# A list scheduler's cost model: landing times that grow with a transfer's size, and time between dependent instructions of one engine

## The chip, the cores and the metric

One core of one Trainium2 chip runs the whole program in one launch. The metric is the device time of that launch in microseconds (us), the median over runs. Engines: PE is TensorE (matmuls), DVE is VectorE, ACT is ScalarE, POOL is GpSimd, and SP is the engine whose queue issues every DMA of this kernel.

## The reference

One layer of a hybrid backbone on 128 context and 1024 latent tokens (1152 rows, NT), model width 1024:

```
mod = silu(c) @ w_mod + b_mod              # 6 x 1024 values: shift, scale, gate of both halves; for c and c_ctx
h   = rmsnorm(x) * (1 + scale_a) + shift_a
z   = h @ w_in                              # 3456 columns: r k v, decay/a/gate LoRA (1920), and 3 x 512 for the convolution
y   = forward and backward RWKV-7 scan (8 heads x 64), group norm, bonus, gate g
oc  = rmsnorm(gate_b * conv3(gate_c * hc))
x1  = x + gate_a * (concat(y, oc) @ w_out)
h2  = rmsnorm(x1) * (1 + scale_f) + shift_f
x2  = x1 + gate_f * (relu(h2 @ w_ff1)**2 @ w_ff2)     # width 4096
out = rmsnorm(x2) * final_g, and the context's final scan states
```

## The kernel before, in words

All the kernel's instructions are emitted through the class `Order`, which is a list scheduler that runs while the program is built. Each piece of work is a generator (a task); an operation that it emits carries the engines it may run on, a modelled duration for each, and the tiles it reads and writes. `start` (L83 to L93) works out the earliest start of an operation from the log of earlier accesses to the same boxes of tiles, adding a latency `HOP` for every pair of different engines; `issue` (L189 on) books it and logs its end plus a `tail`. The scheduler then always takes the operation that can start first, priorities deciding between near-equals. What comes out is one fixed instruction order for each engine, and for a few copies and scalings (`cp`, `mul`, `lin`) also the engine. On the chip each engine runs its order strictly in sequence, with real waits. A model that is wrong therefore costs time as an order in which an instruction stands too early (the engine stands still at it, with everything behind it) or too late.

Of the model, three places matter here: `start`, where an earlier access by the same engine costs nothing; `act` (L335 to L340), an activation's duration from its size; and `dma` (L449 to L451), which books 1.5 us of the queue for 512 KB and a tail of 1900 ns whatever the size.

The program's stages, with the times of the profiled execution:

- A, 0 to 66 us: modulation for the first norm (`mod_in_task`), norm and transposition of x into `hT` (`h_task`).
- B, 66 to 519 us: the input projection. `proj_task` walks over 27 blocks of 128 columns and three groups of 384 rows, 24 matmuls `bank<-hT,w` each. Beside it `front_task`, `value_task`, `kk_task` and `gate_task` turn the results, mostly on DVE and ACT, into scan operands that SP stores to DRAM (`qr_d`, `kb_d`, `kt_d`, `v_d`, `fin_d`). `mod_task` computes the other 32 blocks of the modulation: for each, a load of 512 KB into the only tile `wm`, 16 recorded matmuls `bank<-wm,sc` (eight in the code, in two passes each), a copy to `R`, a small matmul `bank<-sel,R` and an addition; after the last, two copies to `gc`, a transposition, a copy, and the store `gate_d`. The next load of `wm` cannot start before the matmuls on the last one are through.
- C, 519 to 935 us: the scan. `load_task` loads slots (`bk`, `qr`, `V`, `bkT`) of scan operands, `prep_worker` and `chain_task` run short matmuls on 64 x 64 blocks with DVE and ACT between them, `finish_task` normalises (loading `fg` and `f1` from `fin_d`). Its tiles take the place of those of B.
- D, 935 to 1056 us: the output projection (`oproj_task`), and `x1_task`: gate, residual, norm, and eight transpositions `bank<-ident,mx` per tile of 128 rows, each four followed by four `lin` (L400) to `h` on ACT.
- E, 1056 to 1800 us: both matmuls of the MLP.
- Tail, 1800 to 1865 us: the last accumulation of the MLP, and `y_task` per tile of 128 rows: two evacuations `facc<-bank,facc`, times `late` (the gate), plus `late` (x1), a square with accumulation on ACT, `Ln`, `Exp`, and the final scaling (`stt`, L377) with a store.

Of the kernel before, what the change touches and what calls it, by code (L numbers as in the profile page):

```python
# [27 lines left out]
class Order:  # L28
# [9 lines left out]
    HOP = {("pe", "dve"): 205.0, ("pe", "act"): 205.0, ("dve", "pe"): 145.0, ("act", "pe"): 175.0,  # L38
           ("act", "dve"): 150.0, ("dve", "act"): 130.0, ("act", "pool"): 170.0, ("pool", "dve"): 80.0,
           ("dve", "pool"): 150.0, ("pool", "act"): 110.0, ("pool", "pe"): 150.0}  # L40
    SLACK = 20.0
    GLUE = -1.0
    LOAD = 1290.0
# [38 lines left out]
    def start(self, eng, bi, bo, pe=None):  # L82
        t = 0.0  # L83
        if pe:

            t = self.sub + pe[1] * (1 if self.warm(self.sub) else 2)
            t = max([t] + [self.tiles[x] for x in pe[4]])
        for wr, bs in ((False, bi), (True, bo)):
            for nm, p0, p1, f0, f1 in bs:
                for q0, q1, g0, g1, te_, en, w in self.log.get(nm, ()):  # L90
                    if (wr or w or nm in self.banks) and p0 < q1 and q0 < p1 and f0 < g1 and g0 < f1 and en != eng:
                        t = max(t, te_ + self.HOP.get((en, eng), 70.0))
        return t  # L93

    def emit(self, opts, outs, ins, fn, tail=0.0, pe=None, table=None):
# [154 lines left out]
    def run(self, tasks):  # L250
# [3 lines left out]
        while self.tasks:  # L254
# [24 lines left out]
            if not cand:  # L279
# [3 lines left out]
            s0, eng = f.ready[0], f.ready[1]  # L283
            t = min((t for t in cand if t.ready[1] == eng and t.ready[0] <= s0 + self.SLACK),
                    key=lambda t: (t.prio, t.ready[0], t.n))
# [8 lines left out]
            if r != t.ready or n != t.next:  # L294
                t.ready, t.next = r, n
                if r[1] != eng or r[0] > s0 + self.SLACK:
                    continue
# [12 lines left out]
def kernel(  # L310
# [8 lines left out]
    te, ve, se, ge, sy = nc.tensor, nc.vector, nc.scalar, nc.gpsimd, nc.sync  # L319

    od = Order()

    def size(ap):
        n = 1
        for _, c in ap.ap[1:]:
            n *= c
        return n

    def in_psum(ap):
        return ap.space == PSUM  # L330

    def aps(*xs):
        return [x for x in xs if isinstance(x, bass.AP)]

    def act(out, in_, func=AF.Copy, **kw):  # L335
        x = aps(kw.get("scale"), kw.get("bias"))
        d = (52 if in_psum(in_) else 94) + 47 * len(x) + size(in_) / 1.2
        od.emit([("act", d)], [out] + aps(kw.get("accum_out")), [in_] + x,
                lambda e: se.activation(out=out, in_=in_, func=func, **kw),  # L339
                table=TABLES.get(func))  # L340
# [98 lines left out]
    def mm(out, lhsT, rhs, start=True, stop=True, **kw):  # L439
        pe_op(out, lhsT, rhs, lambda e: te.matmul(out, lhsT=lhsT, rhs=rhs, start=start, stop=stop, **kw))  # L440
# [7 lines left out]

    def dma(out, in_):  # L449
        n = size(out) * 4 * out.ap[0][1]  # L450
        od.emit([("dma", max(480.0, n / 350.0))], [out], [in_], lambda e: sy.dma_start(out=out, in_=in_), 1900.0)  # L451

    def split(src, hi, lo, eng="dve"):

# [8 lines left out]
    p1 = ctx.enter_context(tc.tile_pool(name="p1", bufs=1))  # L463
# [30 lines left out]
    for b in bank_t:  # L494
        nm = od.box(b)[0]
# [170 lines left out]
    def split_task():  # L666
        for i in range(2):
            dma(raws[i], w_in[0, :, blocks[i] * 128:(blocks[i] + 1) * 128].rearrange("(k p) c -> p k c", p=128))
        for i, cb in enumerate(blocks):
            if i >= 2:  # L670
                yield lambda: nproj[0] >= i - 1
            w2, raw = w2s[i % 2], raws[i % 2]
            for q in range(4):
                sl = slice(2 * q, 2 * q + 2)
                act(w2[:, 0, sl], raw[:, sl])
                tt(w2[:, 1, sl], raw[:, sl], w2[:, 0, sl].bitcast(F32), ALU.subtract)
            count(nsplit)
            yield
            if i + 2 < len(blocks):
                c2 = blocks[i + 2]  # L680
                dma(raw, w_in[0, :, c2 * 128:(c2 + 1) * 128].rearrange("(k p) c -> p k c", p=128))
# [17 lines left out]
    with tc.tile_pool(name="p0w", bufs=1) as pw, tc.tile_pool(name="p0", bufs=1) as p0:  # L699
# [9 lines left out]
        def par_task(g):  # L709
            r = 0  # L710
            for nm, ap, n in groups[g]:
                src = {"rk": "o (n h) q -> (o n) (h q)", "cw": "o t (n q) -> (o t n) q"}.get(nm, "o (n q) -> (o n) q")
                src = ap.rearrange(src, h=2) if nm == "rk" else ap.rearrange(src, q=128)
                dma(prs[g][r:r + n, :], src)
                r += n
# [5 lines left out]
            if g == 0:  # L721

                for w, nm in ((0, "c"), (1, "cctx")):
                    cv = prm[:, rows[nm]:rows[nm] + 8]
                    t = der[:, 50:58] if w == 0 else der[:, 42:50]
                    act(t, cv, AF.Tanh, scale=0.5)
                    tsc(t, t, 0.5, ALU.mult, 0.5, ALU.add)
                    tt(sc[:, :, w], t, cv, ALU.mult)
                mark(ready, "sc")
            else:  # L730
                yield lambda: "sc" in ready

                r0 = rows["mu"]
                tsc(der[:, 0:15], prm[:, r0:r0 + 15], -1.0, ALU.mult, 1.0, ALU.add)
                tsc(der[:, 15:30], prm[:, r0:r0 + 15], 0.5, ALU.mult)
                r0 = rows["w0_f"]
                tsc(der[:, 30:46], prm[:, r0:r0 + 16], 0.5, ALU.mult)
                r0 = rows["ka"]
                tsc(der[:, 58:62], prm[:, r0:r0 + 4], 0.5, ALU.mult)
                tsc(der[:, 62:66], prm[:, r0:r0 + 4], -0.5, ALU.mult, 1.0, ALU.add)  # L740
                for t, f, b in ((lw_w, w_w2_f, w_w2_b), (lw_a, w_a2_f, w_a2_b)):
                    dma(t[0:64], f[0])
                    dma(t[64:128], b[0])
                dma(lw_g, w_g2[0])
# [13 lines left out]
        def x_task():  # L758
            for i in range(TT):
                dma(xs_t[i], x_rows(i))  # L760
            for a, b in ((0, 5), (5, 9)):
                for i in range(a, b):
                    act(junk, xs_t[i], AF.Square, accum_out=ss[:, 0, i:i + 1])
                act(ss[:, 1, a:b], ss[:, 0, a:b], AF.Ln, scale=1.0 / D, bias=eps[:, 2:3])
                act(ss[:, 1, a:b], ss[:, 1, a:b], AF.Exp, scale=-0.5)
                for i in range(a, b):
                    tsc(xs_t[i], xs_t[i], ss[:, 1, i:i + 1], ALU.mult, eng=("dve", "pool"))
                    mark(ready, ("x", i))
                yield
# [1028 lines left out]
```

## Time and profile before

| what | value |
|---|---|
| median of three runs | 1871.28 us (1868.84, 1871.28, 1874.59) |
| the profiled execution | 1867.13 us, of which the span of the trace is 1865.3 us |
| granted clock of TensorE, mean | 0.981 |
| busy PE / DVE / ACT / POOL | 1725.0 / 1170.3 / 572.9 / 36.0 us |
| share of the 16 DMA engines taken by the queue of SP | 34.5 % |

Busy times are of the span of 1865.3 us. The profiled execution was 4.15 us below the median, so sums that are made against the trace are carried to the median as differences. PE is at work for 92 % of the span, but that is an average over stages: in E it never stops, and in A, in C, at the seams between the stages and in the tail other things end last. Matmul records are modelled, and a few can be missing.

### The profile page before, as it was taken

Reading aid. Unit: us, or ns where it says so; the run is one execution under the profiler, and the core shown is the slowest. Engines: PE = TensorE matmul, PEld = TensorE weight load, DVE = VectorE, ACT = ScalarE, POOL = GpSimd, SP = SyncE. Lnnn points to the kernel's source line nnn. Section 1 sums busy time; section 2 is a strip of 40 time slices with the busy share of each in tenths; the row PEclk is TensorE's granted clock in tenths of the full one; section 3 lists DMA queues with packets and bytes.
Section 4 is the critical chain, followed back from the end, with each engine's and each line's share of the span. In section 5 each row is a group of like instructions: output and inputs, shape, how many; then the busy total and the mean of one; then the engine's idle time right before and its main releaser. Section 6 shows DMA issues by size and latency. Waiting matters only on the chain.

```text
span 1865.3 us, 47366 instructions
## 1 busy us (share of the span) xinstructions
PE 1725.0 (92%) x20250; PEld 1535.8 (82%) x20250; DVE 1170.3 (63%) x2481; ACT 572.9 (31%) x1384; POOL 36.0 (2%) x167
## 2 busy tenths in 40 slices
PE   5899999999877878888989999999999999999996
PEld 3788888988767777777767899999999999999995
DVE  3557676777668877777655534555555555555557
ACT  5444344544244444444334421111100010000112
POOL 6000000000000000000000000000000000000000
PEclk9999999999999999999999999999999999999998
DMA  8436666665544443334144311111111111101142
GB/s 297 112 103 161 167 168 162 157 181 137 135 139 134 143 115 101 101 108 126 58 146 131 102 57 46 46 46 46 46 46 46 45 35 46 38 24 42 46 151 97
DMA packets 291449, 190.35 MB, mean 102 GB/s; under 512 B 109171, under 2 KB 274214, under 8 KB 291238
## 3 DMA queue, kind: packets, MB, share of 16 engines
q1 hardware_dynamic: 291238, 187.32, 34.5%
q8 instruction: 159, 2.61, 0.6%
q14 instruction: 52, 0.43, 0.1%
HBM read 137.44 MB, written 49.82 MB: 100 GB/s over the span
## 4 chain that ended last, share of the span: by engine, by line
PE 72%; DVE 8%; DMA 7%; issue 4%; ACT 4%; SPq 3%; DVEq 0%; ACTq 0%; POOL 0%; POOLq 0%
PE bank L440 72%; SPq L451 3%; DMA wm<-in_w_mod_dram 3%; DVE facc L362 1%; PE bank L443 1%; DMA fg<-fin_d 1%; DVE facc L377 1%; DVE x L362 1%; DVE y L362 1%; ACT mx L339 0%; ACT late L339 0%; DMA raw<-o_d 0%; ACT h L400 0%; DVE mx L362 0%; DMA late<-x_d 0%
## 5 line engine op out<-in xcount | busy, mean ns | idle before, releaser
L440 PE MATMUL bank<-hT,w 128*128 128x384 f32 (+1 forms) x2232 | 448.6, 354 | 0.0
L440 PEld LDWEIGHTS bank<-hT,w 128*128 128x128 f32 x2232 | 395.7, 191 | 26.8 <-issue 10.3
L440 PE MATMUL bank<-h,w 128*128 128x384 f32 x2304 | 409.9, 339 | 0.0
L440 PEld LDWEIGHTS bank<-h,w 128*128 128x128 f32 x2304 | 407.3, 188 | 1.2
L440 PE MATMUL bank<-w2f,f1f 128*128 128x512 f32 x1674 | 385.2, 389 | 0.0
L440 PEld LDWEIGHTS bank<-w2f,f1f 128*128 128x128 f32 x1674 | 314.0, 188 | 64.7
L362 DVE TENSOR_TENSOR facc<-bank,facc 128x512 f32<-128x512 f32 x252 | 173.9, 690 | 134.3 <-PE bank L440 133.1
L339 ACT ACTIVATE rl<-bank 128x384 f32<-128x384 f32 x96 | 47.2, 492 | 340.4 <-PE bank L440 340.4
L362 DVE TENSOR_TENSOR rl<-rl 128x384 f32<-128x384 f32 x96 | 53.4, 557 | 154.9 <-ACT rl L339 154.8
L440 PE MATMUL bank<-qr,bk 64*64 64x128 f32 x1152 | 118.6, 285 | 7.2 <-DMA bk<-kb_d 3.5
L384 ACT ACTIVATE cur<-bank 128x256 f16<-128x256 f32 (+1 forms) x286 | 98.2, 383 | 69.3 <-PE bank L440 56.1
L440 PE MATMUL bank<-cur,at 64*64 64x64 f16 x1728 | 87.0, 196 | 11.3 <-issue 6.5
L440 PEld LDWEIGHTS <-cur 64*64 64x64 f16 x2016 | 76.5, 108 | 24.3 <-issue 19.1
L440 PEld LDWEIGHTS <-at 64*64 64x64 f16 x2016 | 77.6, 108 | 19.9 <-issue 15.2
L440 PE MATMUL bank<-P,cur 64*64 64x64 f16 x1728 | 77.3, 198 | 17.4 <-issue 10.5
L362 DVE TENSOR_TENSOR P<-bank,lmask 128x256 f16<-128x256 f32 x180 | 74.8, 419 | 26.4 <-PE bank L440 22.2
L440 PEld LDWEIGHTS bank<-qr,bk 64*64 64x64 f32 x1152 | 77.6, 137 | 8.3 <-issue 7.9
L362 DVE TENSOR_TENSOR w<-raw,w 128x256 fp32r<-128x256 f32 (+3 forms) x149 | 77.1, 553 | 9.5 <-ACT w L339 7.8
L384 ACT ACTIVATE w2f<-raw 128x1024 fp32r<-128x1024 f32 x11 | 11.7, 1061 | 185.0 <-PE bank L440 184.7
L440 PE MATMUL bank<-G,bk 64*64 64x64 f32 x576 | 59.4, 226 | 3.2 <-issue 3.2
L440 PE MATMUL bank<-qr,Z 64*64 64x64 f32 x576 | 57.2, 223 | 3.4 <-issue 3.4
L440 PE MATMUL bank<-cur,P 64*64 64x64 f16 x1152 | 57.6, 198 | 2.8 <-issue 2.7
(251 smaller groups left out, 2479.9 us busy)
## 6 DMA issues: line engine op xcount, KB each, us to landing
raw<-in_w_ff_dram SPq DMA_DIRECT2D x43, 512.0 KB
wm<-in_w_mod_dram SPq DMA_DIRECT2D x32, 512.0 KB
raw<-in_w_in_dram SPq DMA_DIRECT2D x27, 512.0 KB
rf<-in_w_ff_dram SPq DMA_DIRECT2D x21, 512.0 KB
qr_d<-qr_g SPq DMA_DIRECT2D x24, 384.0 KB
kb_d<-kb_g SPq DMA_DIRECT2D x24, 384.0 KB
kt_d<-kt_g SPq DMA_DIRECT2D x192, 48.0 KB
bk<-kb_d SPq DMA_DIRECT2D x72, 128.0 KB
```

The lines of the kernel that those rows point to most:

```text
L339: lambda e: se.activation(out=out, in_=in_, func=func, **kw),
L362: lambda e: ENG[e].tensor_tensor(out=out, in0=a, in1=b, op=op))
L377: lambda e: ve.scalar_tensor_tensor(out=out, in0=a, scalar=s, in1=b, op0=op0, op1=op1))
L384: lambda e: se.activation(out=out, in_=in_, func=AF.Copy) if e == "act"
L440: pe_op(out, lhsT, rhs, lambda e: te.matmul(out, lhsT=lhsT, rhs=rhs, start=start, stop=stop, **kw))
L443: pe_op(out, in_, identity, lambda e: te.transpose(out=out, in_=in_, identity=identity), 1)
L451: od.emit([("dma", max(480.0, n / 350.0))], [out], [in_], lambda e: sy.dma_start(out=out, in_=in_), 1900.0)
```

## The change

Three edits to the model. In `start`, an earlier write by the same engine now adds `SAME` (115 ns on DVE, 150 on ACT, 100 on POOL) before an instruction that touches what it wrote. In `act`, an activation with `accum_out` is booked 150 ns longer. In `dma`, the tail becomes 1900 ns plus the bytes divided by 200 per ns: for 512 KB 1.9 us becomes 4.5 us, for 192 KB 2.9 us, for 128 KB 2.6 us. No arithmetic is changed; the order of the instructions is, and for some copies the engine. Lines behind the first edit move by 3 to 7 (L362 is L369 after, L377 is L384, L440 is L447, L451 is L458).

```diff
@@ class Order
+    SAME = {"dve": 115.0, "act": 150.0, "pool": 100.0}
@@ start
-                    if (wr or w or nm in self.banks) and p0 < q1 and q0 < p1 and f0 < g1 and g0 < f1 and en != eng:
-                        t = max(t, te_ + self.HOP.get((en, eng), 70.0))
+                    if p0 < q1 and q0 < p1 and f0 < g1 and g0 < f1:
+                        if en != eng:
+                            if wr or w or nm in self.banks:
+                                t = max(t, te_ + self.HOP.get((en, eng), 70.0))
+                        elif w and en in self.SAME:
+                            t = max(t, te_ + self.SAME[en])
@@ act
-        d = (52 if in_psum(in_) else 94) + 47 * len(x) + size(in_) / 1.2
+        d = (52 if in_psum(in_) else 94) + 47 * len(x) + size(in_) / 1.2 + (150 if "accum_out" in kw else 0)
@@ dma
-        od.emit([("dma", max(480.0, n / 350.0))], [out], [in_], lambda e: sy.dma_start(out=out, in_=in_), 1900.0)
+        od.emit([("dma", max(480.0, n / 350.0))], [out], [in_], lambda e: sy.dma_start(out=out, in_=in_),
+                1900.0 + n / 200.0)
```

What it moves, at three places. First, SP's queue at the seam between B and C. Before:

```order
L451 DMA v_d<-vt_g_829 32x6x32 x6
L451 DMA o_d<-oc_851 128x384
L451 DMA fin_d<-gl_g_833 128x384
L451 DMA fin_d<-bt_g_832 128x384
L451 DMA gate_d<-R_801 32x128
L451 DMA v_d<-vt_g_829 32x6x32 x8
L451 DMA fin_d<-gl_g_833 128x384
L451 DMA fin_d<-bt_g_832 128x384
L451 DMA bk_4736<-kb_d 128x256
L451 DMA qr_4733<-qr_d 128x256
```

and after:

```order
L458 DMA v_d<-vt_g_809 32x6x32 x6
L458 DMA wm<-in_w_mod_dram 128x8x128
L458 DMA o_d<-oc_831 128x384
L458 DMA fin_d<-gl_g_813 128x384
L458 DMA fin_d<-bt_g_812 128x384
L458 DMA v_d<-vt_g_809 32x6x32 x8
L458 DMA fin_d<-gl_g_813 128x384
L458 DMA fin_d<-bt_g_812 128x384
L458 DMA wm<-in_w_mod_dram 128x8x128 x2
L458 DMA gate_d<-R_781 32x128
L458 DMA bk_4715<-kb_d 128x256
L458 DMA qr_4712<-qr_d 128x256
```

The last two loads of `wm` and the store `gate_d`, which needs both, now stand between the last store of B and the first load of C; before, all loads of `wm` were issued far ahead, and `gate_d` one tile of values earlier.

Second, PE's order at the same seam, after the change, from the last 24 matmuls of the projection on:

```order
L447 MATMUL bank_94<-hT,w_0_68 128x384 x24
L447 MATMUL bank_97<-bt_g_812,ones_blk 128x384
L447 MATMUL bank_95<-sg_s,lw_g 128x384
L447 MATMUL bank_99<-wm,sc 32x128 x8
L447 MATMUL bank_98<-sel,R_781 128x2
L447 MATMUL bank_96<-bt_g_812,ones_blk 128x384
L447 MATMUL bank_101<-sg_s,lw_g 128x384
L447 MATMUL bank_100<-wm,sc 32x128 x8
L447 MATMUL bank_94<-sel,R_781 128x2
L447 MATMUL bank_97<-wm,sc 32x128 x8
L447 MATMUL bank_95<-sel,R_781 128x2
L450 MATMUL bank_99<-ident,gc 32x128
```

Three blocks of the modulation and the transposition of `gc` now come behind the projection; before, all of them stood among its matmuls. Earlier in B the other blocks have moved too: between the `sel,R` of one block and the `wm,sc` of the next, fewer than 4 us of other matmuls stood at 13 of the 32 blocks, and stand at 6.

Third, DVE in the tail. Before (`facc` is the accumulator, `late9` the gate, `late1` and `late2` are x1 of a tile, `late11` the final gain, banks are results of PE):

```order
L377 SCALAR_TENSOR_TENSOR facc_17188<-facc_17188,sf_17187,late11_21766 128x1024
L362 TENSOR_TENSOR facc_17188<-bank7_101,facc_17188 128x512
L362 TENSOR_TENSOR facc_17188<-facc_17188,late9_21764 128x1024
L362 TENSOR_TENSOR facc_17188<-facc_17188,late1_21756 128x1024
L362 TENSOR_TENSOR facc_17188<-bank2_96,facc_17188 128x512
L377 SCALAR_TENSOR_TENSOR facc_17188<-facc_17188,sf_17187,late11_21766 128x1024
```

and after:

```order
L369 TENSOR_TENSOR facc_17167<-bank3_97,facc_17167 128x512
L369 TENSOR_TENSOR facc_17167<-facc_17167,late1_21735 128x1024
L369 TENSOR_TENSOR facc_17167<-bank6_100,facc_17167 128x512
L369 TENSOR_TENSOR facc_17167<-facc_17167,late9_21743 128x1024
L384 SCALAR_TENSOR_TENSOR facc_17167<-facc_17167,sf_17166,late11_21745 128x1024
```

Between the addition of `late1` and the final scaling of that tile stood one evacuation; now there stand an evacuation and the multiplication of the next tile by `late9`.

## Rows read from the trace of the kernel before

**Rows 1.** The first part of the page, the engines' busy time with its share of the span and its instructions.

```profile
PE 1725.0 (92%) x20250; PEld 1535.8 (82%) x20250; DVE 1170.3 (63%) x2481; ACT 572.9 (31%) x1384; POOL 36.0 (2%) x167
```

**Rows 2.** Busy time of each engine in five stretches, the tail from 1812 us on and the stages B, C, D and E: stretch, its length, then busy us and instructions of each engine, the granted clock of PE, the share of the DMA engines, and GB/s.

```profile
1812.00:1865.30 53.30, 37.54 (x166) 30.76 (x164) 40.57 (x43) 13.57 (x35) 0.00 (x0) 0.88 0.34 136
...
66.00:519.00 453.00, 431.31 (x2682) 385.39 (x2682) 309.01 (x675) 191.41 (x421) 2.61 (x24) 0.97 0.56 146
519.00:935.00 416.00, 345.51 (x12636) 305.72 (x12636) 320.21 (x952) 185.30 (x576) 1.15 (x8) 0.98 0.40 113
935.00:1056.00 121.00, 112.85 (x542) 91.58 (x542) 67.34 (x108) 50.01 (x125) 0.00 (x0) 0.97 0.41 135
1056.00:1800.00 744.00, 744.00 (x3783) 684.47 (x3783) 394.43 (x616) 89.66 (x148) 0.00 (x0) 1.00 0.14 43
```

**Rows 3.** A wait of PE at the start of B, in the order of time of its instructions: start, duration, engine, line, operation, count, and in brackets the idle time before it with its releaser.

```profile
66.07 0.59 PE L440 MATMUL bank<-sel,R 128*128 128x2 f32 x2 [3.35 <-ACT R L384]
```

**Rows 4.** All that PE waited for between 100 and 505 us, in B: total us, times, longest us.

```profile
PE bank L440 <- DMA wm<-in_w_mod_dram: 14.3, 16, 2.8
```

**Rows 5.** PE in order of time behind two of these waits (columns as in rows 3), a short one at 229 us and one of 2.27 us at 377 us.

```profile
229.99 0.78 PE L440 MATMUL bank<-hT,w 128*128 128x384 f32 x3
230.61 0.28 PE L440 MATMUL bank<-sel,R 128*128 128x2 f32 x2
...
377.44 0.64 PE L440 MATMUL bank<-wm,sc 128*32 128x128 f32 x16 [2.27 <-DMA wm<-in_w_mod_dram]
378.02 1.12 PE L440 MATMUL bank<-hT,w 128*128 128x384 f32 x3
```

**Rows 6.** Pieces of the chain of work that ended last in which the load of a `wm` block is the link: start us, us from its issue to its landing.

```profile
425.13 3.93 DMA wm<-in_w_mod_dram
...
430.02 5.86 DMA wm<-in_w_mod_dram
...
480.44 4.23 DMA wm<-in_w_mod_dram
```

**Rows 7.** SP's queue at the seam between B and C, in order of time: start, us, the transfer, count.

```profile
509.52 0.44 SPq L451 DMA_DIRECT2D gate_d<-R  x1
...
517.35 0.38 SPq L451 DMA_DIRECT2D fin_d<-bt_g  x1
519.42 0.32 SPq L451 DMA_DIRECT2D bk<-kb_d  x1
```

**Rows 8.** PE at the same seam (columns as in rows 3).

```profile
484.71 1.08 PE L440 MATMUL bank<-wm,sc 128*32 128x128 f32 x16 [2.81 <-DMA wm<-in_w_mod_dram]
...
486.85 0.42 PE L440 MATMUL bank<-sel,R 128*128 128x2 f32 x2
...
512.51 1.65 PE L440 MATMUL bank<-bt_g,ones_blk 128*128 128x384 f32 x2 [6.00 <-DVE bt_g L377]
...
522.34 1.97 PE L440 MATMUL bank<-qr,bk 64*64 64x128 f32 x16 [3.51 <-DMA bk<-kb_d]
```

**Rows 9.** Waits in C, 519 to 935 us, of PE and of DVE: total us, times, longest us.

```profile
PE bank L440 <- issue: 42.1, 55, 1.8
...
DVE y L362 <- DMA fg<-fin_d: 3.4, 5, 1.1
...
DVE y L362 <- DMA f<-fin_d: 1.9, 1, 1.9
```

**Rows 10.** D, 935 to 1060 us: all that PE waited for in front of the transpositions of `mx` (total us, times, longest us), and what ACT stood at during the longest of these waits (columns as in rows 3).

```profile
PE bank L443 <- DVE mx L371: 4.4, 7, 1.3
PE bank L443 <- ACT h L400: 3.7, 1, 3.7
...
969.62 0.31 ACT L384 ACTIVATE hT<-raw 128x128 fp32r<-128x128 f32 x1 [4.78 <-DMA raw<-o_d]
```

**Rows 11.** The tail as the chain of work that ended last goes through it, one tile of 128 rows: start us, us, what.

```profile
1813.41 0.61 DVE facc L362
1814.04 1.24 DVE facc L362
1815.30 1.24 DVE facc L362
1816.56 1.16 ACT late L339 x2
...
1818.30 1.28 DVE facc L377
```

**Rows 12.** DVE's waits for ACT in the tail, 1810 us to the end: total us, times, longest us.

```profile
DVE facc L377 <- ACT sf L339: 8.8, 8, 1.2
```

**Rows 13.** The end of the tail: the start of a half tile of PE, PE's last half tile, and three of DVE's last groups (columns as in rows 3).

```profile
1803.14 2.20 PE L440 MATMUL bank<-w2f,f1f 128*128 128x512 f32 x9
...
1846.66 2.20 PE L440 MATMUL bank<-w2f,f1f 128*128 128x512 f32 x9
1848.70 0.84 PE L440 MATMUL bank<-w,f1f 128*128 128x512 f32 x3
...
1856.81 0.68 DVE L362 TENSOR_TENSOR facc<-bank,facc 128x512 f32<-128x512 f32 x1
1857.53 1.42 DVE L362 TENSOR_TENSOR facc<-facc,late 128x512 f32<-128x512 f32 x2
1860.49 1.28 DVE L377 SCALAR_TENSOR_TENSOR facc<-facc,sf,late 128x1024 f32<-128x1024 f32 x1 [0.60 <-ACT sf L339]
```

## The prediction

> **What bounds the kernel now.** The page's first part comes first: PE is busy for 1725.0 of 1865.3 us [rows 1], so what an order can win is in the 140 us in which PE stands. The busy times by stage say where these are [rows 2]: E stands for 0 of 744 us, B for 22 of 453, D for 8 of 121, C for 70 of 416, and in the tail DVE, with 40.6 of 53.3 us, is busier than PE. PE runs the same matmuls in the same order in E, so E is worth nothing whatever is rearranged beside it. Next come the waits, stage by stage, because they name what ends last. In B, PE waits 16 times, 14.3 us in all, for the load of a `wm` block [rows 4]. In D it waits 4.4 us for `mx` and once 3.7 us for ACT [rows 10]. In the tail DVE waits 8.8 us for the chain of square, `Ln` and `Exp` [rows 12]. In C most of PE's standing has no releaser that shows (42.1 us of "issue") [rows 9].
>
> **Part by part.** All three edits only reorder, so each place where the order moved is priced, in the order of the program.
>
> *A.* PE waits 3.35 us for a copy to `R` early in B [rows 3]; in the new order a few projection matmuls stand in front of it. The copy comes late because ACT is full there, so I count 1 us of gain, between 0 and 3.35 less, and 2 us more if the reshuffled ACT work is later.
>
> *B, the waits for `wm`.* The old model expected a load to be there 3.4 us after its issue (1.5 for the queue, 1.9 behind it), the new one 6.0. The trace shows 3.93, 5.86 and 4.23 us [rows 6]: nearer to the new model in its worst case, and never as short as the old. The Trainium skill, DMA: Bandwidth & Descriptors, "Anatomy of one DMA", fits a fixed 2.0 us plus the bytes over 436 GB/s, measured on another issuing engine, which by estimate is 3.2 us for 512 KB; by it the old tail would have been right, the new one would only push work later, and this term would be 0. The rows disagree with it by 0.7 us and more. The order now leaves under 4 us of other matmuls between a block and the next at 6 places where there were 13, so of the 14.3 us I take 7/13 as gained, 7.7 us; bounds 0 and 14.3. A long wait also costs clock: behind the one of 2.27 us three `hT,w` matmuls take 1.12 us, behind the shorter one 0.78 us [rows 5]. Behind the longest, of 2.81 us, `wm,sc` takes 1.08 us for 0.64 and `sel,R` 0.42 for 0.28 [rows 5, 8], 0.6 us more. For four waits over 1 us I add 2 us. Sum: 9.7 us gained.
>
> *B, three blocks fewer inside.* Three blocks leave PE's stream, each 0.64 us of `wm,sc` [rows 5] and 0.28 us of `sel,R` [rows 5]: 2.8 us gained there.
>
> *The seam, where these blocks go.* In SP's queue the last two `wm` loads and `gate_d` now stand ahead of the first `bk` of C. Before, the first `bk` was issued 2.1 us after the last `fin_d` (519.42 against 517.35), and PE began C at 522.34 [rows 7, 8]. Now, after that `fin_d`: a load of 4.23 us [rows 6], matmuls of 1.08 us, as behind the long wait at 484.71 [rows 8], and the same again, since there is one `wm` tile and the second load waits for the first matmuls. That is 10.6 us. Then the copy to `R`, `sel,R` and its addition: 1.5 us from the end of `wm,sc` at 485.79 to the end of `sel,R` at 487.27 [rows 8]. Then two copies, a transposition, a copy and the store, of which no row stands alone; I take as much again, 1.5 us, an estimate from the pair before. That is 13.6 us in place of the 1.6 or so that `bk` waited anyway: **12 us lost**. Nothing covers it, since PE has only the three `sqs` matmuls left. Bounds: 8 (each load 3.93, its matmuls at full clock, the end of the chain beside other waits) and 17 (both loads 5.86). `gate_d` is not needed before D; it is only its place in the queue that costs.
>
> *C.* Both orders have 72 chain steps with about the same work between them. What the new landing time can take away is DVE's 3.4 us for `fg` and 1.9 us for `f` [rows 9]; what a reshuffle can do to 70 us of standing is bounded only by their size. I take 1 us of gain, between a gain of 6 and a loss of 8, a tenth of the standing time either way.
>
> *D.* The wait of 3.7 us came from ACT, which stood 4.78 us at a copy that needs a load of `o_d`, with the scalings of `h` behind it [rows 10]. In the new order most scalings of the first tile stand in front of that copy, so this wait goes, but for a remainder. The transpositions of later tiles come a few matmuls later, which covers waits of up to 1.3 us each, 4.4 in all [rows 10]. I take 4.5 of the 8.1 us; bounds 1 and 8.
>
> *E.* 0: PE stands for nothing [rows 2]. ACT takes 18 casts more in 744 us, of which it is busy for 90.
>
> *Tail.* One tile took 6.18 us on DVE: 0.61, 1.24, 1.24, 0.61 and 1.28 of work and 1.2 of waiting [rows 11]. From the end of the addition at 1816.54 to the scaling at 1818.30 ACT needs 1.76 us [rows 11], and one evacuation of 0.61 covered a third of it. Seven such waits and a last one make the 8.8 us [rows 12]. With an evacuation and a multiplication between, 1.85 us, the chain is just covered from the second tile on. DVE then needs 5.0 us a tile, and what decides is PE: half a tile takes 2.72 us (1803.14 to 1846.66 is 16 of them), so a tile 5.44 us, and the last bank is ready at 1849.54 [rows 13]. The last evacuation, at 1856.81 before, comes at 1849.6 or, behind the multiplication, 1850. Behind it the new order has one addition (0.7) and one scaling (1.28) more than before, which gives back 2 us. **5.3 us gained**; bounds 3 (cover just missed) and 7.1 (six whole waits).
>
> The sum: -1 - 9.7 - 2.8 + 12 - 1 - 4.5 - 5.3 = -12.3, from 1867.1 to 1854.8 us for the profiled execution. That execution was 4.15 us under the median, so against 1871.28 the forecast is **1859 us**, 0.66 % less.
>
> **The rivals.** *The landing time is not what B waited for.* If loads are late because `wm` stands behind eight `kt_d` stores in SP's queue, or the fit of the page above is nearer than the three rows, the waits stay: B gives 2.8, the seam takes 12, C nothing, D 2, the tail 5.3. That is +2, about 1873 us. Against it speaks that the rows count from the issue, behind the queue, and still exceed 3.4 us [rows 6].
>
> *Slower: the first load of C behind the modulation.* The end of B hangs on DVE and SP rather than on PE: PE waits 6.0 us for `bt_g` at 512.51 [rows 8]. So PE's gain in B may not reach the last `fin_d`, while the seam's 12 to 17 us are paid in full, and D and the tail return 5 to 9. At a seam of 15, no gain from B, D at 1 and the tail at 5.3 it is +9, 1880 us. It decides from the point where less than half of B's 12.5 us arrives at the last `fin_d`.
>
> *Only the tail.* B's gain and the seam cancel and D and C move by their noise: -5.3, 1866 us.
>
> *More.* All of B's waits go (14.3, with 3 of clock and the 2.8), the seam takes 10, C and D give 5 each and the tail 6: -26, 1845 us.
>
> **How the numbers follow.** Chances: the forecast 0.43, more 0.15, only the tail 0.12, waits that stay 0.17, slower 0.13. A measurement can tell some 0.3 % from no change, 5.6 us. Faster by more: 0.43 + 0.15 + half of the tail's case, 0.64. Within: the other half and the case at 1873, 0.23. Slower by more: 0.13. The range runs from the case of "more" at 1845 to 1876, past the case at 1873; most of the slower case is left out.
>
> **What would show it.** Right: PE's waits for `wm` in B under 8 us; the last `wm` matmuls after the projection, with PE standing for over 12 us before the first `qr,bk` of C, on a load of `bk`, behind `gate_d`; one wait of 1.2 us at the scaling in the tail instead of seven, and PE's last matmul closer to the end of the span by some 5 us; no wait for `h` on ACT in D. Wrong would be an unchanged total of waits for `wm`, a seam under 8 or over 17 us, a tail that still takes 6.18 us a tile, or a C that differs by more than 8 us.

## The result, and the profile after

The changed kernel takes 1825.6 us (1822.73 to 1832.81, four runs) against 1871.72 for the kernel before: a ratio of 0.976, 95 % interval 0.9727 to 0.9792, so 46 us faster. The forecast was 1859, the range ended at 1845. The sign was right and the size was not: nearly four times the gain.

The profiled execution took 1824.81 us with a span of 1823.0, 42.3 us less than before. Seven milestones of the two traces, each the first or last record of one kind of instruction, say where these went:

| stretch | before | after | difference | forecast |
|---|---|---|---|---|
| start to first projection matmul (A) | 62.1 | 61.1 | -1.0 | 0 |
| first to last projection matmul (B) | 442.8 | 412.4 | -30.4 | -13.5 |
| to the last store `fin_d<-bt_g` | 12.4 | 15.0 | +2.6 | 0 |
| to the first `qr,bk` of C (the seam) | 5.0 | 19.0 | +14.0 | +12 |
| to the last `qr,Z` of the chain (C) | 408.0 | 399.3 | -8.7 | -1 |
| to the first transposition of `mx` | 34.5 | 29.5 | -5.0 | in C |
| to the first matmul of the MLP (D) | 84.0 | 75.9 | -8.1 | -4.5 |
| to the last matmul `w2f,f1f` of the MLP (E) | 799.7 | 799.5 | -0.2 | 0 |
| to the end (tail) | 16.8 | 11.3 | -5.5 | -5.3 |

The wait for `R`, for which the prediction took 1 us under A, comes at 66 us, behind the first projection matmul, so its term stands in the row of B. The 1.0 us of the first row says nothing of the edits: a second trace of the changed order has 58.2 us there.

What PE waited for inside the projection, 61 to 474 us after (total us, times, longest us; it answers to [rows 3, 4]):

```profile
PE bank L447 <- ACT kk_j L346: 0.9, 3, 0.5
```

All of the 14.3 us for `wm` are gone from the projection, and the 3.35 us for `R` with them. Waits for `wm` there still are: the three blocks that moved behind the projection cost PE 5.9, 6.7 and 3.4 us, two of them in the seam below. What the waits inside the projection had cost besides stands in the granted clock. Busy time by stretch (the columns of [rows 2]), before:

```profile
62.00:100.00 38.00, 34.65 (x231) 32.14 (x223) 16.08 (x41) 10.13 (x28) 0.15 (x2) 0.91 0.26 73
150.00:200.00 50.00, 47.58 (x286) 44.84 (x285) 39.60 (x84) 19.60 (x47) 0.44 (x4) 0.97 0.72 182
350.00:400.00 50.00, 47.73 (x286) 45.21 (x286) 38.23 (x81) 19.57 (x45) 0.44 (x4) 0.97 0.71 183
485.00:505.00 20.00, 20.00 (x114) 19.51 (x107) 14.91 (x31) 2.96 (x8) 0.00 (x0) 0.85 0.50 122
```

and after, the same stretches and the end of the projection:

```profile
61.00:100.00 39.00, 39.00 (x289) 35.69 (x287) 18.79 (x50) 10.41 (x29) 0.15 (x2) 1.00 0.38 108
150.00:200.00 50.00, 50.00 (x321) 46.86 (x319) 39.19 (x83) 19.63 (x48) 0.33 (x3) 1.00 0.73 186
350.00:400.00 50.00, 49.51 (x282) 44.35 (x280) 37.91 (x77) 23.16 (x52) 0.54 (x5) 1.00 0.68 169
440.00:474.00 34.00, 34.00 (x204) 31.83 (x203) 27.48 (x54) 13.49 (x30) 0.11 (x1) 1.00 0.72 166
```

A clock of 0.91 over 38 us is 0.09 x 38 = 3.4 us of PE work that was not done; the four stretches lose 3.4, 1.5, 1.5 and 3.0, together 9.4 us, and each goes with one of the four longest stalls (3.35, 2.42, 2.27 and 2.81 us); some 0.9 of the first 3.4 us lies in the stall itself, where the clock had already fallen (0.77 from 62.10 to 66.07 us). After the change no stretch of the projection is below 1.00. So of the 30.4 us some 18 are standing, some 9 the clock, and some 2 the blocks that left (in this stretch 31 blocks of the modulation stand before and 29 after, since one that ran ahead of it now runs inside); the last 1 to 2 us are not assigned.

The seam, SP's queue after (it answers to [rows 7]):

```profile
488.54 0.38 SPq L458 DMA_DIRECT2D fin_d<-bt_g  x1
489.01 5.96 SPq L458 DMA_DIRECT2D wm<-in_w_mod_dram  x2
502.33 0.34 SPq L458 DMA_DIRECT2D gate_d<-R  x1
504.52 0.35 SPq L458 DMA_DIRECT2D bk<-kb_d  x1
```

and PE there (it answers to [rows 8]; `[...]` is the idle time before, with its releaser):

```profile
493.45 1.08 PE L447 MATMUL bank<-wm,sc 128*32 128x128 f32 x16 [6.73 <-DMA wm<-in_w_mod_dram]
494.98 0.59 PE L447 MATMUL bank<-sel,R 128*128 128x2 f32 x2 [0.46 <-ACT R L391]
...
498.97 1.08 PE L447 MATMUL bank<-wm,sc 128*32 128x128 f32 x16 [3.40 <-DMA wm<-in_w_mod_dram]
500.49 0.59 PE L447 MATMUL bank<-sel,R 128*128 128x2 f32 x2 [0.45 <-ACT R L391]
501.63 0.37 PE L450 MATMUL bank<-ident,gc 128*32 128x128 f32 x1 [0.55 <-DVE s L384]
...
507.53 3.35 PE L447 MATMUL bank<-qr,bk 64*64 64x128 f32 x32 [1.69 <-DMA bk<-kb_d]
```

Two loads one after the other, their matmuls at 1.08 us, `gate_d`, and only then the first `bk`, 16.0 us after the last `fin_d` where it was 2.1.

In D, PE's waits (912 to 1020 us; they answer to [rows 10]) fell from 8.1 to 1.6 us:

```profile
PE bank L450 <- DVE mx L378: 1.4, 3, 0.5
PE bank L450 <- ACT h L407: 0.2, 1, 0.2
```

The tail, DVE over one tile (it answers to [rows 11]):

```profile
1792.94 1.28 DVE L384 SCALAR_TENSOR_TENSOR facc<-facc,sf,late 128x1024 f32<-128x1024 f32 x1
1794.14 0.68 DVE L369 TENSOR_TENSOR facc<-bank,facc 128x512 f32<-128x512 f32 x1
1794.74 1.21 DVE L369 TENSOR_TENSOR facc<-facc,late 128x1024 f32<-128x1024 f32 x1
1796.51 0.69 DVE L369 TENSOR_TENSOR facc<-bank,facc 128x512 f32<-128x512 f32 x1 [0.56 <-PE bank L447]
1797.24 1.23 DVE L369 TENSOR_TENSOR facc<-facc,late 128x1024 f32<-128x1024 f32 x1
1798.38 1.28 DVE L384 SCALAR_TENSOR_TENSOR facc<-facc,sf,late 128x1024 f32<-128x1024 f32 x1
```

and all its waits for ACT at the scaling, 1770 us to the end (they answer to [rows 12]):

```profile
DVE facc L384 <- ACT sf L346: 1.8, 2, 1.2
```

The period is 5.44 us a tile in place of 6.18, and what DVE waits for now is PE. That is the step as it was worked out.

### The profile page after: what moved, and what is told of

It reads as the page before. It is cut to its first block, busy times and chain, and to the rows that moved or that the text cites. A ratio compares the mean times of both kernels' runs of the same rounds, so it can differ in the third digit from the quotient of the medians.

```text
span 1823.0 us, 47295 instructions
## 1 busy us (share of the span) xinstructions
PE 1709.5 (94%) x20229; PEld 1527.6 (84%) x20229; DVE 1156.5 (63%) x2467; ACT 570.4 (31%) x1398; POOL 37.5 (2%) x167
## 4 chain that ended last, share of the span: by engine, by line
PE 61%; DVE 3%; issue 3%; DMA 2%; ACT 1%; SPq 0%; DVEq 0%; ACTq 0%
PE bank L447 60%; DMA raw<-o_d 1%; PE bank L450 1%; DMA qr<-qr_d 1%; SPq L458 0%; DVE y L369 0%; DVE P L369 0%; DVE facc L369 0%; ACT cur L391 0%; DVE bk L384 0%; ACT h L407 0%; DMA o_d<-y 0%; DVE x L369 0%; DVE mx L369 0%; ACT mx L346 0%
## 5 line engine op out<-in xcount | busy, mean ns | idle before, releaser
L447 PE MATMUL bank<-hT,w 128*128 128x384 f32 (+1 forms) x2232 | 440.3, 349 | 0.0
L447 PE MATMUL bank<-h,w 128*128 128x384 f32 x2304 | 410.0, 339 | 0.0
L447 PEld LDWEIGHTS bank<-hT,w 128*128 128x128 f32 x2232 | 388.2, 188 | 25.7 <-issue 9.2
L447 PEld LDWEIGHTS bank<-h,w 128*128 128x128 f32 x2304 | 407.3, 188 | 1.2
L447 PE MATMUL bank<-w2f,f1f 128*128 128x512 f32 x1674 | 385.2, 389 | 0.0
L447 PEld LDWEIGHTS bank<-w2f,f1f 128*128 128x128 f32 x1674 | 314.0, 188 | 64.7
L369 DVE TENSOR_TENSOR facc<-bank,facc 128x512 f32<-128x512 f32 x252 | 174.2, 691 | 138.7 <-PE bank L447 138.7
L369 DVE TENSOR_TENSOR rl<-rl 128x384 f32<-128x384 f32 x96 | 53.6, 558 | 165.0 <-ACT rl L346 164.9
L447 PE MATMUL bank<-qr,bk 64*64 64x128 f32 x1152 | 114.7, 284 | 5.5 <-issue 2.8
L447 PEld LDWEIGHTS <-cur 64*64 64x64 f16 x2016 | 75.2, 107 | 21.9 <-issue 16.3
L447 PE MATMUL bank<-cur,at 64*64 64x64 f16 x1728 | 83.0, 195 | 7.2 <-issue 4.8
L447 PEld LDWEIGHTS <-at 64*64 64x64 f16 x2016 | 75.8, 108 | 15.2 <-issue 11.1
L369 DVE TENSOR_TENSOR w<-raw,w 128x256 fp32r<-128x256 f32 (+3 forms) x149 | 78.3, 553 | 13.7 <-ACT w L346 8.5
L447 PE MATMUL bank<-P,cur 64*64 64x64 f16 x1728 | 75.8, 197 | 11.9 <-issue 7.0
L369 DVE TENSOR_TENSOR P<-bank,lmask 128x256 f16<-128x256 f32 x180 | 73.7, 419 | 19.1 <-PE bank L447 16.3
L447 PEld LDWEIGHTS bank<-qr,bk 64*64 64x64 f32 x1152 | 77.7, 137 | 7.1 <-issue 6.8
L447 PE MATMUL bank<-qr,Z 64*64 64x64 f32 x576 | 56.1, 223 | 5.5 <-issue 5.5
L447 PE MATMUL bank<-cur,P 64*64 64x64 f16 x1152 | 56.2, 199 | 4.7 <-issue 4.6
L447 PE MATMUL bank<-G,bk 64*64 64x64 f32 x576 | 55.6, 223 | 3.6 <-issue 3.6
```

Of the source, the lines that this page charges most:

```text
L369: lambda e: ENG[e].tensor_tensor(out=out, in0=a, in1=b, op=op))
```

## The experiments

Every kernel was timed against the kernel before on the chip it ran on, where that took 1859 to 1864 us. The stretches are those of the table above; "projection" is its second row.

**The three edits, one at a time.** Each alone, in the diff's own words:

```diff
# e1_landing_only
-  ... lambda e: sy.dma_start(out=out, in_=in_), 1900.0)
+  ... lambda e: sy.dma_start(out=out, in_=in_), 1900.0 + n / 200.0)
# e2_same_only
+    SAME = {"dve": 115.0, "act": 150.0, "pool": 100.0}      # and its use in start
# e3_accum_only
-        d = ... + size(in_) / 1.2
+        d = ... + size(in_) / 1.2 + (150 if "accum_out" in kw else 0)
```

> Only the landing time grows with the size; the other two edits are left out. Theory 1 (the landing time is what empties B of its waits): no wait for a wm block inside the projection, so that the stretch from the first to the last projection matmul shrinks from 443 to about 412 us as in the changed kernel; five wm blocks instead of three come behind the projection, three of them and gate_d behind the last fin_d, so the first qr,bk of C comes about 3 x 5.3 + 3 = 19 us later than without them; tail and D as before; in all about -12 us, 1860 us. Rival (time between dependent instructions does it, by taking DVE and ACT results earlier): the waits for wm stay near 14 us and the seam still loses, 1880 us or more.

> Only the time between dependent instructions of one engine. Theory 1: B keeps some 14 us of waits for wm and its low clock (stretch of the projection 435 to 445 us), the seam is as before (first qr,bk 5 us after the last fin_d), the tail gains 5.5 us, C and D gain what they gained in the changed kernel, 12 and 8 us: about 1847 us. Rival (C and D gain from loads that are used later, by the landing time): only the tail gains, 1866 us.

> Only the 150 ns more for an activation with accumulation. Both theories: two or three of the seven waits of 1.18 us in the tail go (the order covers the chain of ACT for some tiles only), 3 us; the rest as before, up to the noise of a reshuffled C: 1868 us.

| kernel | time | ratio (interval) | projection | to `fin_d` | seam | C | to `mx` | D | tail |
|---|---|---|---|---|---|---|---|---|---|
| landing only | 1838.94 | 0.988 (0.9864 to 0.9903) | 417.1 | 17.4 | 24.4 | 397.2 | 30.7 | 76.6 | 17.0 |
| `SAME` only | 1835.09 | 0.987 (0.9845 to 0.9888) | 434.2 | 17.8 | 5.0 | 400.9 | 31.2 | 78.9 | 12.3 |
| accumulation only | 1849.65 | 0.994 (0.9916 to 0.9963) | 439.5 | 13.5 | 5.0 | 404.8 | 34.7 | 81.3 | 12.8 |

The places divide as theory 1 had it. With the landing time alone PE waits 0.8 us for `wm` inside the projection; with `SAME` alone it is this, 57 to 520 us (columns as in [rows 4]):

```profile
PE bank L447 <- DMA wm<-in_w_mod_dram: 16.2, 16, 4.8
PE bank L447 <- DVE bt_g L384: 11.5, 1, 11.5
```

Sixteen waits as before. The landing time also makes the seam, 24.4 us, the 19 more that were expected. The tail comes from `SAME`; the accumulation's edit alone gives most of it too, 4 us, more than the 3 expected, and the whole kernel gained 9.6 us by it, not 3. What neither theory had is that the landing time alone shortens C and D, by 11 and 7 us, so that it gives 20 us, not 12. `SAME` alone shortens them by 7 and 5 us, as its theory had it in part (12 and 8). The accumulation's 3 us in C are within what a mere reshuffle moves (below). `SAME` alone was expected at 1847 on the first chip, 0.987, and gave 0.987, but partly from other places: its projection is some 8 us shorter with all the waits for `wm` still there. The wait for `R` is not among its waits any more, and its clock is 1.00 from 150 to 200 and from 350 to 400 us.

**The seam undone in the changed kernel.** The modulation's task ranks higher, so that its blocks are done early:

```diff
-  (2, mod_task(), 2),
+  (0.5, mod_task(), 2),
```

> The changed kernel with the modulation's task at priority 0.5 instead of 2, so that its last block is done before the last quarter of the projection and gate_d is stored far ahead of the seam. Theory (the seam costs 14 us because the first loads of C stand behind wm, wm and gate_d in SP's queue): first qr,bk about 5 us after the last fin_d instead of 19, so 1812 us. Rival (the seam is set by DVE's last values and by tiles of C that take the place of those of B, and the wm loads only fill it): no gain, 1825 us, or a loss where wm loads collide with other loads inside B again.

1821.31 us, 0.979 (0.9768 to 0.9810): no gain over the changed kernel's 0.976 to 0.979 (and 1820.98 us, on the same chip, with the nudge of 2 ns below). The seam did go, from 19 to 5.4 us. But the projection took 420.1 us for 412.4, and from its end to the last `fin_d` 21.0 us passed for 15.0. The rival had it: PE stood there for the values' chain instead (waits of PE, 57 to 520 us),

```profile
PE bank L447 <- DVE bt_g L384: 14.6, 1, 14.6
PE bank L447 <- issue: 3.7, 1, 3.7
PE bank L447 <- DMA wm<-in_w_mod_dram: 1.8, 2, 1.2
```

so this order shows the seam's cost removed and given back, not that it was never there.

**Both kernels once more on one chip.** No edit.

> The kernel before once more, on the chip of the runs beside it, for its stages. Theory (the stages' differences come from the edits): the scan C near 408 us, projection near 443, D near 84 as in its first profile. Rival (chips differ, and part of what the single edits seemed to gain in C and D is the chip): C near 404, D near 81, as in the run with the accumulation's edit alone, which moved hardly anything there.

> The changed kernel once more beside the others. Both theories: 0.976 of the kernel before, give or take 0.004; first qr,bk 19 us after the last fin_d.

Before: projection 441.3, C 407.6, to `mx` 34.2, D 84.1, tail 16.9, in all 1867.38 us (one run). After: 413.7, seam 18.9, C 399.4, to `mx` 29.1, D 75.0, tail 11.3; 1823.12 us, 0.9785 (0.9752 to 0.9818). From the projection on, the stages of the same order repeat within 2 us here (A differed by 2.9 us), so most of the differences belong to the orders and not to the chip. The single edits ran on another chip than these two; D there is covered by the nudges below, 83.9 and 85.0 us on that chip without any of the three edits, and C by their 408.3 and 403.2.

**A smaller landing time.** The size's term divided by 300 and by 250 instead of 200:

```diff
# e7_landing_third
-                1900.0 + n / 200.0)
+                1900.0 + n / 300.0)
# e12_landing_fourth
+                1900.0 + n / 250.0)
```

> The changed kernel with a landing time of 1900 ns plus bytes over 300 instead of 200 (5.1 us in all for 512 KB instead of 6.0). The order then has one wm block behind the projection, its load ahead of the last v_d stores, and gate_d ahead of the last fin_d. Theory (5.1 still covers nearly all landings, and the seam's cost is the place of wm and gate_d in SP's queue): waits for wm inside the projection under 4 us, first qr,bk 5 to 7 us after the last fin_d, 10 us faster than the changed kernel. Rival (with the seam's stall gone the values' chain on DVE and SP ends as late): the gain at the seam comes back as a longer time from the last projection to the last fin_d, no difference from the changed kernel.

> The changed kernel with bytes over 250 instead of 200 in the landing time (5.5 us in all for 512 KB). In its order no wm block stands behind the projection and gate_d far ahead of the seam. Theory (between 5.1, which let 6.5 us of waits for wm back in, and 6.0, which pushed blocks behind the projection, lies a value with neither): waits for wm under 3 us in the projection, first qr,bk 5 us after the last fin_d, projection 415 us, 1812 us or 0.972. Rival (blocks that fit inside the projection without waits lengthen it, or the end hangs on the values' chain): no better than the third, 1813 to 1818.

With 300: 1813.11 us, 0.973 (0.9699 to 0.9769), 10 us under the changed kernel beside it (its profiled execution, 1817.66 us, was the slowest of four). The seam is 5.2 us, because `gate_d` is ahead of the last `fin_d` in SP's queue:

```profile
479.72 0.40 SPq L458 DMA_DIRECT2D wm<-in_w_mod_dram  x1
...
490.97 0.38 SPq L458 DMA_DIRECT2D gate_d<-R  x1
491.45 0.37 SPq L458 DMA_DIRECT2D fin_d<-gl_g  x1
491.91 0.38 SPq L458 DMA_DIRECT2D fin_d<-bt_g  x1
494.00 0.32 SPq L458 DMA_DIRECT2D bk<-kb_d  x1
```

The time to the last `fin_d` stays at 15.2 us, so here the rival is wrong and the seam's cost is real: its 13.7 us come back, less 6 us of a longer projection (419.6). With 250: 1811.96 us, 0.972 (0.9700 to 0.9743); waits for `wm` 0.6 us, projection 416.7, seam 5.0. (The 6.5 us of waits with 300 that the expectation names are 0.8 inside the projection and 5.7 at the block behind it.) The two can't be told apart, and both beat the changed kernel. In the kernel before, thirteen loads of `wm` blocks lie on the chain of work that ended last between 100 and 500 us; they landed 3.8 to 5.9 us after their issue, eleven of them in under 5.1 us. The landing time that serves here is one that covers most of them, not the one on the safe side.

**The clock by itself.** In the kernel before, dummy matmuls go ahead of the four instructions behind the longest stalls of B; their bank is overwritten right after:

```diff
+    FILL_W, FILL_R = {26: 22, 40: 21, 47: 26}, {16: 31}      # block: number of matmuls of 128x256, f16
+            for _ in range(n):
+                te.matmul(bank[:, 0:256]..., lhsT=ident16, rhs=ident16..., start=True, stop=True)
```

> The kernel before with dummy matmuls (128x256, f16, some 0.11 us each, on a bank that is overwritten right after) ahead of four instructions at which PE stood for 2.3 to 3.4 us in B: the wm blocks at 180, 377 and 485 us (22, 21 and 26 of them) and the sel,R at 66 us (31); nothing else is moved. Theory (behind each such stall PE runs at the lower clock for several us, 9.6 us of lost work in all, which was the larger part of what I had missed in B): the granted clock in B stays at 1.00 and B ends 6 to 9 us earlier, the rest as before: ratio 0.996. Rival (the stalls cost their own length only): no gain, 0 to 1 us slower.

1854.96 us, 0.995 (0.9927 to 0.9972): faster with 100 matmuls more and nothing moved. The stretches of its projection, to be read against those of before above:

```profile
62.00:100.00 38.00, 37.44 (x290) 33.90 (x290) 16.96 (x44) 11.46 (x30) 0.15 (x2) 1.00 0.29 83
150.00:200.00 50.00, 49.68 (x315) 46.79 (x314) 39.85 (x84) 19.97 (x47) 0.44 (x4) 1.00 0.74 190
350.00:400.00 50.00, 49.96 (x316) 47.08 (x316) 37.84 (x80) 19.89 (x46) 0.33 (x3) 1.00 0.69 171
480.00:500.00 20.00, 19.14 (x119) 17.72 (x118) 14.82 (x31) 2.96 (x8) 0.00 (x0) 1.00 0.50 125
```

The clock stays at 1.00 and the projection takes 434.3 us, 7.0 less than the same order without fillers on that chip (441.3), where the first three stretches lost 6.4 us by their clock (0.91, 0.97 and 0.97 there too). The first `qr,bk` came 5.5 us earlier. That much is shown; that its C was shorter as well (402.3 for 407.6, same order) is not explained by it, so of the 0.5 % only the projection's 7.0 us are the clock's.

In that repeat of the kernel before, the fourth stall did not bring the clock down: PE stood 2.84 us, and the stretch behind it ran at 1.00, where the same place had 0.85 in the first profile.

```profile
486.24 0.64 PE L440 MATMUL bank<-wm,sc 128*32 128x128 f32 x16 [2.84 <-DMA wm<-in_w_mod_dram]
...
485.00:505.00 20.00, 18.76 (x118) 17.73 (x118) 14.81 (x31) 2.96 (x8) 0.00 (x0) 1.00 0.54 141
```

**How much a mere reshuffle moves.** Nudges of the model that say nothing about the chip but reorder C:

```diff
# e9_before_nudged_5ns: in the kernel before
-  ... sy.dma_start(out=out, in_=in_), 1900.0)
+  ... sy.dma_start(out=out, in_=in_), 1905.0)
# e10_before_nudged_2ns in the kernel before, e11_after_nudged_2ns in the changed one
-    HOP = {("pe", "dve"): 205.0, ...
+    HOP = {("pe", "dve"): 207.0, ...
```

> The kernel before with a landing time of 1905 instead of 1900 ns: a nudge that says nothing about the chip, but reshuffles the order of DVE from its row 1118 on, in C; A, B and the tail stay. Theory (C and D gain from what the edits say): C 403 to 408 us, D 84, in all within 0.3 % of the kernel before. Rival (any reshuffle of C draws a time, and the kernel before had drawn a poor one): C or D move by 4 us or more, either way.

> The kernel before with a hop from PE to DVE of 207 instead of 205 ns, a second such nudge; the order of DVE changes from its row 715 on, late in B and in C. Theory: C 403 to 408 us and D 84 again, within 0.3 %. Rival: another draw, 4 us or more from the first.

> The changed kernel with the same nudge of 2 ns in the hop from PE to DVE; its order of DVE changes from row 1043 on. Theory: C within 2 us of 399, D of 76, 0.978 of the kernel before. Rival (C's gain in the changed kernel was a lucky draw): C 402 to 408 us, 0.980 to 0.983.

| kernel | time | ratio (interval) | C | clock in C | to `mx` | D |
|---|---|---|---|---|---|---|
| before, 5 ns | 1861.14 | 0.999 (0.9974 to 1.0006) | 408.3 | 0.97 | 29.3 | 83.9 |
| before, 2 ns | 1855.40 | 0.997 (0.9951 to 0.9982) | 403.2 | 0.98 | 29.8 | 85.0 |
| changed, 2 ns | 1820.98 | 0.977 (0.9760 to 0.9789) | 395.9 | 1.00 | 31.2 | 74.9 |

D stays at 84 to 85 before and 75 to 76 after: its gain is the edits'. The 5 us from the end of the chain to the first `mx` are not: both nudges of the kernel before win them. C lies at 402 to 408 us in the five traces whose order is that of the kernel before or a nudge of it (and at 404.8 with the accumulation's edit alone). It lies at 396 to 399 in the three of the changed kernel, and at 397 to 402 in the five others that have the landing time, `SAME` or both. The means are 405.7 and 398.9 us: some 7 us are the edits', and some 3 us either way are the draw. The clock does not order these lengths: it is 0.97 at 402.3 us (fillers) and 0.97 at 408.3.

## Why the prediction was wrong

*The tail* was right to 0.2 us, in its mechanism (an evacuation and a multiplication cover ACT's chain) and in its second bound, PE at 5.44 us a tile. *The seam* was right too: 14.0 us for 12, two loads, their matmuls at 1.08 us and `gate_d`, in that order; two fits of the landing time that empty that place win 10 and 9 us over a changed kernel on the same chip. *E* was 0.

*B's waits* failed in their size, and twice. First, the step "at 6 places where there were 13, so of the 14.3 us I take 7/13 as gained" measured a wait by the matmuls between a block and the next. The waits did not stand there. By the trace's times seven blocks, not thirteen, had under 4 us of such work ahead of them; even the thirteen with the least held only some 4 of the 14.3 us, and the three longest stalls, 7.5 us, came behind 35 to 40 us of it. In SP's queue their loads stood behind stores of `kt_d` and `v_d`, and PE was ready for them 1.5 to 3.0 us after the issue. The first of them in the kernel before, on PE,

```profile
142.66 0.28 PE L440 MATMUL bank<-sel,R 128*128 128x2 f32 x2
...
180.05 0.88 PE L440 MATMUL bank<-wm,sc 128*32 128x128 f32 x16 [2.42 <-DMA wm<-in_w_mod_dram]
```

in SP's queue and, as in [rows 6], from issue to landing:

```profile
169.05 3.91 SPq L451 DMA_DIRECT2D kt_d<-kt_g  x8
...
174.60 1.36 SPq L451 DMA_DIRECT2D wm<-in_w_mod_dram  x1
...
174.60 5.40 DMA wm<-in_w_mod_dram
```

After the change the load behind the same stores is used 6.5 us after its issue, and nothing waits:

```profile
169.19 1.42 SPq L458 DMA_DIRECT2D wm<-in_w_mod_dram  x1
...
175.69 0.64 PE L447 MATMUL bank<-wm,sc 128*32 128x128 f32 x16
```

So the new landing time works on the distance from a load's issue to its use, also where the PE work between two blocks is long, and inside the projection it took all 14.3 us and not 7.7. Second, **the clock**: the 2 us "for four waits over 1 us" stood for 6.0 behind three of these (the one of 1.05 us at 414 us was followed by 1.00), and for the 3.4 us that go with the wait for `R` there was no term. I had priced it by the two instructions right behind a wait [rows 5, 8], while the clock stays down for several us more: over the 20 us behind the last stall it was 0.85 on average. The fillers confirm it, 7.0 us of projection with nothing moved. The two steps missed about as much, 6.6 us of waits and 7.4 of clock. The Trainium skill, TensorE: Matmul & The Clock Gate, "HAM oscillation", tells of a kernel in which every wait for a DMA is followed by matmuls at the lower of the two levels. This trace agrees for three of its sixteen waits for `wm`, those of 2.27 to 2.81 us; behind the others, 1.05 us at most, the clock stayed at 1.00.

*The wait for `R`.* Its 3.35 us were counted at 1, under A, and all went.

*D* was sized 4.5 for 8.1: by PE's busy time in that stretch 6.3 us of standing for the 4.5, and the clock for the rest (0.98 over 84 us before, 1.00 after: 1.7 us), again the term that I had left out.

*C* was put at 1 us, between a gain of 6 and a loss of 8, and is the largest miss of a single term: it gave 8.7, beyond the 8 us that the prediction named as a sign of being wrong, and 5.0 behind it. The 5.0 us are chance, since both nudges of the kernel before win them too: it had drawn a slow passage from C to D. Of the 8.7 us some 7 are the edits' and the rest the draw. Which wait of C brings them is not settled: with either edit alone C shrinks (397.2 and 400.9 us), and DVE's waits for `fg` and `f`, 5.3 us in all [rows 9], are 2.0 after. But with the nudge of 2 ns in the kernel before they are 7.4 us, and its C is 403.2.

By the same rows the rival "the landing time is not what B waited for" is out: the landing time alone takes these waits from 14.3 to 0.8 us. That rival was right that the longest stalls' loads stood behind `kt_d` stores; what it had wrong is that the waits would stay. With a model of 5.1 or 5.5 us for such a load nearly nothing waits inside the projection any more, at 3.4 sixteen blocks did. The 3.2 us for 512 KB that the prediction estimated from the Trainium skill, DMA: Bandwidth & Descriptors, "Anatomy of one DMA", are below all thirteen landings counted above (3.8 us and more).

The range failed with the forecast because its lower end was made of the same terms: "more" took 3 us of clock, and C at 5.

## What to carry to other kernels

Price a long stall of TensorE with the clock that follows it: multiply what the granted clock lacks of 1.00 by the length of the stretch behind it, not the slowness of the next two instructions. Measure a load's slack from its issue in its queue to its use, not from the use before. In a list scheduler, a duration that is too short makes an engine stand at a place too early for it, and one that is too long pushes work to where nothing covers it; both showed here, and the best value lay between. Before a gain in a reordered stage is ascribed to an edit, nudge the model by a few ns: what that moves is the draw.

## What the runs showed of the hardware that was not expected

In the projection, where the DMA engines were busy for 56 % of the time [rows 2], the thirteen loads of 512 KB counted above landed 3.8 to 5.9 us after their issue, and a model of 5.1 us was enough to cover all but 0.8 us of PE's waits inside the projection. In the first profile, each stretch of 20 to 50 us around or behind one of four stalls of 2.3 to 3.4 us ran at a mean clock of 0.85 to 0.97, which cost 1.5 to 3.4 us, about as much as the stall. In the fourteen traces of this case PE stood 22 times for 2.1 to 4.9 us inside the projection, and with 21 of these stalls the granted clock fell to its lower level (0.50 of the full one) for some us; with nine stalls of 1.3 to 1.7 us it never did. 100 dummy matmuls of 0.11 us in the place of the stalls shortened the projection by 7.0 us.
